# The first feed-forward block of a hybrid encoder: x loaded by token halves, the first products' operands made first, and the weight sums issued in another order

## The chip, the cores and the metric

The kernel runs on one core of a Trainium2 chip. The metric is the device time of one execution in microseconds (us), lower is better. TensorE (PE in the profile) multiplies, ScalarE (ACT) and VectorE (DVE) work elementwise, GpSimd (POOL) here only issues DMAs, and SyncE (SP) issues the plain loads.

## The reference, cut to what matters

The reference is a trunk of two layers over 512 tokens and 16 learned meta tokens (T = 528), model width 1024, float32. Each layer is half a feed-forward block, a mixer of gated linear attention and grouped-query attention, and another half block:

```python
def rmsnorm(x, g):
    xf = x.astype(jnp.float32)
    y = xf * lax.rsqrt(jnp.mean(xf * xf, axis=-1, keepdims=True) + EPS)
    return (y * g.astype(jnp.float32)).astype(x.dtype)

def swiglu(x, w_gate, w_up, w_down):
    return (jax.nn.silu(x @ w_gate) * (x @ w_up)) @ w_down
...
    for l in range(DEPTH):
        h = h + 0.5 * swiglu(rmsnorm(h, norm_gains[l, 0]),
                             ffn_w_gate[l, 0], ffn_w_up[l, 0], ffn_w_down[l, 0])
        h = h + mixer(rmsnorm(h, norm_gains[l, 1]), w_in[l], ...)
        h = h + 0.5 * swiglu(rmsnorm(h, norm_gains[l, 2]),
                             ffn_w_gate[l, 1], ffn_w_up[l, 1], ffn_w_down[l, 1])
    return rmsnorm(h, final_norm)[:, N_META:]
```

Only the start of the first `swiglu` (layer 0, block 0; the hidden width is 2816) is touched here.

## The kernel before, in words

The residual stream `h` lies in SBUF with channels on partitions: eight chunks of 128 channels by 528 tokens. Every float32 product is made of three matmuls on split values: an operand v becomes hi = v rounded to the PE's reduced float32 (a cast on ACT) and lo = v - hi (a subtraction on DVE), and hi·hi, hi·lo and lo·hi are added up in PSUM. For weights these are `whi` (line L290 of the program before, L304 after) and `wlo` (L291, L305).

Gate and up projections of a feed-forward block go by a scheme that needs seven block products instead of eight. The 22 hidden tiles of 128 form 11 pairs, the 8 chunks of channels form 4 pairs, and the 528 tokens two halves of 264. A product "(p, c)" below is product number c of hidden pair p: 24 matmuls of 128x264 (4 channel pairs, 2 columns, 3 splits). Products "1", "2" and "4" use the weight blocks W11, W12 and W22 as they are, loaded by SP; the others use sums of blocks: "7" uses s3 = W21 - W11, "6" uses s2 = W22 + s3, "5" uses s1 = W21 + W22, "3" uses s4 = s2 - W12. For the first pairs of a block (`OPENING` and those that `chained` names) the sums are made by the memory system: a negation on ACT or a plain load puts the first block into a tile of 512 KB, and an accumulating DMA that POOL issues (`add`, L209 before, L212 after) adds the other one. s2 needs s3, so its add waits for the add of s3, and s4's waits for that of s2. An engine's instructions run in the order in which they are written; an add whose tile isn't ready holds up every later add on POOL.

The products of the first block run in the order (0,1), (0,2), (1,1), (1,2), (0,4), (1,4), (0,6), (0,5), (0,7), and then (0,3), (1,6) and (1,5), of which before runs (1,6) and seven matmuls of (1,5) ahead of (0,3).

The operand side needs seven combinations of the two channel halves (b11, b12 of one chunk, b21, b22 of the other; the second index is the token half): b11 for product "1", b21 for "2", b12 - b11 and b22 - (b12 - b11) for "5" and "6", and so on, the one in place 5 for product "4". `Norm.pair` makes all seven for one channel pair in one go: two scaled copies of h (L512), the casts of the seven (L519) and their low parts (L520). The norm's division is made later: the squares of h (`square`, L502) are summed on DVE (L506), multiplied by a matrix of constants on PE (`means`, L474), and a reciprocal root follows on ACT and DVE (`rsqrt_of`); its result scales the hidden tiles (L651). `snapshot` (L605, L615) copies a PSUM accumulator to SBUF on ACT.

In before, x comes in chunk by chunk and pair by pair, with `pair(0)` to `pair(3)` and the first four weight blocks made in turn:

```python
    first.pair(0)
    W.fetch(1)
    for c in (2, 4, 6):
        nc.sync.dma_start(hall[:, c : c + 2], xt[:, c : c + 2])
    W.make(1)
    W.fetch(2)
    first.pair(1)
```

The functions that the change touches are these, with the line numbers of the profile.

Of the kernel before, what the change touches and what calls it, by code (L numbers as in the profile page):

```python
# [146 lines left out]
    return cols, -(-col // SLAB)  # L147


NPAIR = FF // P // 2  # L150
NOP = NPAIR + QUADS * FAST
PLAN = weight_plan()
# [19 lines left out]
class Weights:  # L172
# [3 lines left out]
    def __init__(self, tc, raw, hi, lo, wts, win):  # L176
        nc = tc.nc
        self.tc, self.nc, self.raw, self.hi_pool, self.lo_pool, self.wts, self.win = tc, nc, raw, hi, lo, wts, win
        self.long = self.short = None
        self.loads = []  # L180
        for t, col in zip(PLAN, COLUMN):
            if t[0] == "op":
                self.loads.append(t[1:])
            elif col % SLAB == 0:
                self.loads.append(col // SLAB)
        self.at = {load: i for i, load in enumerate(self.loads)}
        self.made, self.fetched, self.got, self.summed, self.raws = 0, 0, {}, {}, {}
        self.pos = 0
        self.behind = None

    def dram(self, f, i, name):
        return self.win[((f[0] * 2 + f[1]) * NOP + i) * 4 + ("11", "12", "21", "22").index(name)]

    def block(self, f, i, name, pool=None, tag="raw"):

        w = (pool or self.raw).tile([P, SLAB], F32, tag=tag, name=f"w{name}_{f[0]}{f[1]}_{i}")
# [9 lines left out]

    def add(self, t, src):

        self.nc.gpsimd.dma_start(t, src, accum_op=ALU.add)  # L209

    def chained(self, f, i):
        return i < 2 or f == (0, 0) and i < 4  # L212
# [1 line left out]
    def begin_sums(self, f, i, w=None):  # L214

        got = self.summed
        s3 = None
        if self.chained(f, i):
            s3 = self.negative(f, i, "s3", w)
            self.add(s3, self.dram(f, i, "21"))  # L220
        elif i < NPAIR:
            s3 = self.block(f, i, "21", self.long, "wsa")
        s2 = self.block(f, i, "22", self.short, "wsb")
        if self.chained(f, i):
            self.add(s2, s3)
        got[f, i, "7"], got[f, i, "6"] = s3, s2
        if (f, i) not in OPENING:
            self.first_sum(f, i)

    def first_sum(self, f, i):  # L230
        s1 = self.block(f, i, "21", self.short, "wsb")
# [3 lines left out]
    def sums(self, f, i, product, w):  # L235


        got, V = self.summed, self.nc.vector
        if (f, i) in OPENING and product in "12":
            (self.begin_sums if product == "1" else self.first_sum)(f, i, *[w] * (product == "1"))  # L240
        if i < 2:
            if product == "2":
                s4 = self.negative(f, i, "s4", w)
                self.add(s4, got[f, i, "6"])
                got[f, i, "3"] = s4
        elif product == "1" and not self.chained(f, i):
            if i < NPAIR:
                self.kept1 = w
            else:
                got[f, i, "7"] = self.negative(f, i, "s3", w)  # L250
                self.add(got[f, i, "7"], self.dram(f, i, "21"))
                self.add(got[f, i, "6"], got[f, i, "7"])
        elif product == "2":
            self.kept = w
            if i < NPAIR and not self.chained(f, i):
                V.tensor_tensor(got[f, i, "7"], got[f, i, "7"], self.kept1, ALU.subtract)
        elif product == "6":
            s4 = self.long.tile([P, SLAB], F32, tag="wsa", name=f"s4_{f[0]}{f[1]}_{i}")
            V.tensor_tensor(s4, w, self.kept, ALU.subtract)
            got[f, i, "3"] = s4  # L260

    def fetch(self, upto):

        while self.fetched < min(upto, len(self.loads)):
            load = self.loads[self.fetched]
            if isinstance(load, int):
                w = self.raw.tile([P, SLAB], F32, tag="raw", name=f"raw{load}")
                self.nc.sync.dma_start(w, self.wts[load])
                self.raws[self.fetched] = w
            elif load[2] in DIRECT:  # L270
                self.raws[self.fetched] = self.block(*load[:2], DIRECT[load[2]])
# [4 lines left out]
    def make(self, upto):  # L276
        nc = self.nc
        while self.made < min(upto, len(self.loads)):
            self.fetch(self.made + 1)
            s = self.made  # L280
            load = self.loads[s]
            w = self.raws.pop(s, None)
            if w is None:
                w = self.summed.pop(load)
            hi = self.hi_pool.tile([P, SLAB], F32R, tag="whi", name=f"whi{s}")
            lo = self.lo_pool.tile([P, SLAB], F32R, tag="wlo", name=f"wlo{s}")
            for a in np.split(np.arange(SLAB), 2 if s == 0 else 1):
                cs = slice(a[0], a[-1] + 1)
                with self.tc.issue_after(self.behind) if self.behind else nullcontext():
                    nc.scalar.copy(hi[:, cs], w[:, cs])  # L290
                nc.vector.tensor_tensor(lo[:, cs], w[:, cs], hi[:, cs].bitcast(F32), ALU.subtract)  # L291
            self.got[s] = (hi, lo)
            self.got.pop(s - 12, None)
            self.made += 1
            if not isinstance(load, int) and load[2] in "126":
# [36 lines left out]
def build(tc, ctx, xt, wts, win, par, w2, const, umask, out):  # L332
# [155 lines left out]
    class Norm:  # L488


        def __init__(self, gc):
            self.gc, self.x, self.acc = gc, [], None

        def operand(self, c):
            hi, lo = slot("x", F32R), slot("x", F32R)
# [12 lines left out]
        def pair(self, j):  # L508
# [23 lines left out]
            parts(slice(4, 6), v2(t34))  # L532
            self.x.append((hi, lo))

        def chunk(self, c):
            self.operand(c)
            self.square(c)
# [35 lines left out]

    pending = [load_constants]

    def ffn(l, f, norm, done, following):

        x, rs, up, n = norm.x, None, None, live[0]
        w = n // 2
# [177 lines left out]
        for i, step in enumerate(steps):  # L757
            if step[0] == "P":
                if step[1:] == (0, "5") and norm.acc is None:
                    for c in range(KC):  # L760
                        norm.square(c)
                product_of_pair(*step[1:])
                if step[1:] == (0, "5"):
                    rs, up = norm.rs(True)
                    W.behind = prev_act[0]
                if step[1] in (2, 3) and step[2] in "6574":
                    m = next(risen)
                    V.scalar_tensor_tensor(h(m), h(m), -1.0, up, ALU.mult, ALU.mult)
                if i == last_op:
                    close_pools(norm.pools)  # L770
                    following()
            elif step[0] == "S":
                fast_down(*step[1:])
            elif step[0] == "O":
                g, last = step[1:]
                ks = slice(3, 4) if last else slice(0, 3)
                operands_of(g, ks, "152")
                difference(g, 0, 3, 0, ks)
                if last:
                    operand(g, "6")  # L780
            else:
                down(*step[1:])
        close_pools(pools)

    def project(x, rs, tag, f=1.0, n=T):
# [445 lines left out]
    def ending(sums, operand, rs):  # L1231
# [43 lines left out]
        factor(1)  # L1275
        leave(1, (0, 2, 4, 6))

    first = Norm(G_NORM)
    operand_pools(first, "xc")
    bp = [block_pools()]  # L1280
    nc.sync.dma_start(h(1), xt[:, 1])
    first.pair(0)
    W.fetch(1)
    for c in (2, 4, 6):
        nc.sync.dma_start(hall[:, c : c + 2], xt[:, c : c + 2])
    W.make(1)
    W.fetch(2)
    first.pair(1)
    W.make(2)
    W.fetch(3)  # L1290
    first.pair(2)
    W.make(3)
    W.fetch(4)
    first.pair(3)
    nc.sync.dma_start(ct[:, C_O1024 : C_O1024 + P], const[:, C_O1024 : C_O1024 + P])

    norms = [first] + [Norm(G_NORM + i * KC) for i in range(1, 3 * DEPTH)]
    for l in range(DEPTH):
        a, b, c = norms[3 * l : 3 * l + 3]
        ffn(l, 0, a, b.chunk, lambda: operand_pools(b, "x"))  # L1300
# [79 lines left out]
```

## Time and profile before

| | us |
|---|---|
| median of 3 runs | 2196.76 (2196.46 to 2197.05) |
| the profiled execution, whole | 2196.04 |
| its span | 2194.3 |
| PE busy in it | 2157.0 (98%) |
| DVE busy | 1777.9 (81%) |
| ACT busy | 1215.5 (55%) |
| POOL busy | 105.3 (5%) |
| mean granted PE clock | 0.998 |

The span runs from the first to the last instruction of the profiled execution; the execution's own time is 1.7 us longer. A row of a timeline reads: start, duration, engine, line, operation, result <- operands, shapes, count, and in brackets how long the engine was idle before it and what ended that wait.

### The profile page before, as it was taken

What the parts mean: (1) busy time and instruction counts of PE and PEld (TensorE: products, weight loads), DVE (VectorE), ACT (ScalarE), POOL (GpSimd) and SP (SyncE); (2) the same over time, 40 slices, a digit from 0 to 9 for tenths busy, and PEclk for the clock granted to TensorE, in tenths of its full rate; (3) what the DMA queues carried; (4) which work ended last, traced back from release to release, by engine and by line L of the source; (5) the groups of instructions that cost most, each with busy time, mean ns of one, the idle gap of its engine ahead of it and who ended that gap; (6) DMA issues with size and microseconds to landing.
All of it is one profiled execution on the core that took longest, in us unless ns stands there. A gap on an engine that the chain in (4) does not pass through costs nothing.

```text
span 2194.3 us, 40087 instructions
## 1 busy us (share of the span) xinstructions
PE 2157.0 (98%) x16506; PEld 2066.7 (94%) x16506; DVE 1777.9 (81%) x2699; ACT 1215.5 (55%) x1781; POOL 105.3 (5%) x124
## 2 busy tenths in 40 slices
PE   7999999999999999999999999999999999999998
PEld 7999999989999999999999999999788888999997
DVE  7887977586976689788799879785878767997987
ACT  8545545354784556454575455453557836554543
POOL 1100000000000000010010000000000001000100
PEclk9999999999999999999999999999999999999999
DMA  9866743212113567676667667432121145776752
GB/s 282 218 194 184 200 125 111 78 49 68 49 39 120 129 176 182 202 182 184 165 164 186 198 181 203 127 109 80 49 78 49 49 134 151 197 202 181 195 161 68
DMA packets 87751, 312.46 MB, mean 142 GB/s; under 512 B 9744, under 2 KB 12176, under 8 KB 87568
## 3 DMA queue, kind: packets, MB, share of 16 engines
q1 hardware_dynamic: 68336, 244.48, 33.6%
q0 software_dynamic: 17280, 62.92, 16.1%
q10 hardware_dynamic: 1952, 2.50, 0.4%
q8 instruction: 130, 2.13, 0.4%
q14 instruction: 53, 0.43, 0.1%
HBM read 289.94 MB, written 2.10 MB: 133 GB/s over the span
## 4 chain that ended last, share of the span: by engine, by line
PE 76%; DVE 16%; ACT 4%; issue 2%; DMA 2%; SPq 0%; POOL 0%; DVEq 0%; ACTq 0%
PE ss L601 33%; PE mm L468 13%; PE ss L721 11%; PE ss L468 10%; DVE wlo L291 4%; PE sm L468 2%; DVE g L687 1%; PE sm L1083 1%; DVE c L683 1%; DVE g L683 1%; PE ss L1058 1%; DVE c L651 1%; DMA w<-win 1%; DVE g L661 1%; PE ss L474 1%
## 5 line engine op out<-in xcount | busy, mean ns | idle before, releaser
L601 PE MATMUL ss<-xc,whi 128*128 128x264 f32 (+1 forms) x4928 | 903.4, 285 | 11.6 <-ACT whi L290 7.4
L601 PEld LDWEIGHTS ss<-xc,whi 128*128 128x128 f32 x4928 | 764.8, 189 | 14.9 <-ACT whi L290 7.8
L601 PE MATMUL ss<-xc,wlo 128*128 128x264 f32 (+1 forms) x2464 | 700.7, 285 | 3.4 <-DVE wlo L291 3.3
L601 PEld LDWEIGHTS ss<-xc,wlo 128*128 128x128 f32 x2464 | 465.1, 189 | 5.2 <-DVE wlo L291 5.2
L291 DVE TENSOR_TENSOR wlo<-w,whi 128x1024 fp32r<-128x1024 f32 (+1 forms) x335 | 405.5, 1217 | 64.1 <-ACT whi L290 63.9
L290 ACT CAST whi<-w 128x1024 fp32r<-128x1024 f32 (+1 forms) x335 | 345.9, 1048 | 159.8 <-PE ss L601 80.3
L468 PE MATMUL mm<-x,whi 128*128 128x264 f32 (+1 forms) x1712 | 384.8, 315 | 0.0
L468 PEld LDWEIGHTS mm<-x,whi 128*128 128x128 f32 x1712 | 278.4, 188 | 16.6 <-issue 1.0
L468 PE MATMUL mm<-x,wlo 128*128 128x264 f32 (+1 forms) x856 | 266.1, 315 | 0.0
L721 PE MATMUL ss<-g,whi 128*128 128x264 f32 (+1 forms) x1280 | 237.0, 284 | 0.0
L290 ACT CAST whi<-raw 128x1024 fp32r<-128x1024 f32 x126 | 132.1, 1049 | 163.5 <-PE mm L468 102.7
L605 ACT COPY c<-ss 128x528 f32<-128x528 f32 (+1 forms) x132 | 78.5, 595 | 245.7 <-PE ss L601 245.3
L291 DVE TENSOR_TENSOR wlo<-raw,whi 128x1024 fp32r<-128x1024 f32 x126 | 153.9, 1222 | 59.3 <-ACT whi L290 58.4
L721 PEld LDWEIGHTS ss<-g,whi 128*128 128x128 f32 x1280 | 198.4, 188 | 0.1
L721 PE MATMUL ss<-g,wlo 128*128 128x264 f32 (+1 forms) x640 | 181.3, 283 | 0.0
L468 PEld LDWEIGHTS mm<-x,wlo 128*128 128x128 f32 x856 | 159.6, 188 | 8.5 <-issue 0.7
L468 PE MATMUL ss<-g,whi 128*128 128x264 f32 (+2 forms) x900 | 166.2, 299 | 0.0
L468 PEld LDWEIGHTS ss<-g,whi 128*128 128x128 f32 x900 | 131.7, 188 | 5.2
L209 POOL DMA_DIRECT2D w<-win x60 | 52.7, 879 | 1557.1 <-DVE t L1211 392.2
L721 PEld LDWEIGHTS ss<-g,wlo 128*128 128x128 f32 x640 | 120.5, 188 | 0.0
L447 ACT ACTIVATE c<-c 128x528 f32<-128x528 f32 (+1 forms) x88 | 56.5, 642 | 96.3 <-DVE c L651 96.1
L291 DVE TENSOR_TENSOR wlo<-s,whi 128x1024 fp32r<-128x1024 f32 x86 | 104.9, 1220 | 1.7 <-ACT whi L290 1.5
(268 smaller groups left out, 3374.0 us busy)
## 6 DMA issues: line engine op xcount, KB each, us to landing
w<-win SPq DMA_DIRECT2D x333, 512.0 KB, 4.5
raw<-wts SPq DMA_DIRECT2D x126, 512.0 KB, 3.3
w<-win POOLq DMA_DIRECT2D x60, 512.0 KB, 7.4
s<-win POOLq DMA_DIRECT2D x26, 512.0 KB, 7.6
w<-s POOLq DMA_DIRECT2D x26, 512.0 KB, 6.0
s<-w POOLq DMA_DIRECT2D x8, 512.0 KB, 8.0
h<-xt SPq DMA_DIRECT2D x3, 528.0 KB, 6.6
out<-h ACTq DMA_DIRECT2D x4, 256.0 KB, 2.4
```

What stands on the lines that cost most here:

```text
L209: self.nc.gpsimd.dma_start(t, src, accum_op=ALU.add)
L290: nc.scalar.copy(hi[:, cs], w[:, cs])
L291: nc.vector.tensor_tensor(lo[:, cs], w[:, cs], hi[:, cs].bitcast(F32), ALU.subtract)
L447: prev_act[0] = S.activation(*args, **kw).ins
L468: TE.matmul(acc.half[i][:width], lhs, rhs[:, acc.spans[i]], start=first, stop=last)
L474: TE.matmul(a, weights, x[:, hs], start=True, stop=True)
L601: TE.matmul(acc[:, j], a[:, j, k], b[:, at], start=bool(begin and k == 0 and i == 0), stop=k == len(x) - 1 and i == 2, skip_group_check=no ...
L605: W.behind = S.copy(part(st, q), acc).ins
L651: V.scalar_tensor_tensor(td, ts, -0.5, rs[:, cs], ALU.mult, ALU.mult)
L661: V.tensor_tensor(raw[p // 4][2 * m + q][:, p % 4], t[:, q * w : (q + 1) * w], us, ALU.mult)
L683: V.tensor_tensor(lo, src[:, ks], hi.bitcast(F32), ALU.subtract)
L721: TE.matmul(acc[:, j], a[:, j, k], xs[b][:, k], start=bool(begin and k == 0 and i == 0), stop=k == 3 and i == 2, skip_group_check=not begin)
```

## The change

Four things are changed, all at the program's start.

- x is loaded by token halves: the first half of channels 0 and 1, then of the others, then the second halves. `Norm.pair` is replaced for this block: `head(j)` makes the operands of products "1" and "2" of a pair (from the first half of the tokens, two half-width activations that are the cast themselves), `fourth(j)` that of product "4", `middle(j)` and `rest(j)` the others. The heads of all four pairs come first; the others are called from `between`, after given steps of the product loop.
- Three early blocks (W12 of pair 1, W22 of pairs 0 and 1) go into spare tiles of another pool ("g"), and W22 of pair 0 for the second sum is loaded ahead, behind x.
- The sums of the two opening pairs are made by `open_sums`, with the second add kept ahead of the next pair's first one (`issue_after`); the negations are made when products "1" and "2" are.
- `warm_up(5)` runs five float32 matmuls on a tile of zeros ahead of everything.

```diff
@@ class Weights
+    def open_sums(self, f, i):
+        got = self.summed
+        with self.tc.issue_after(self.added) if self.added else nullcontext():
+            self.add(got[f, i, "7"], self.dram(f, i, "21"))
+        s2 = got[f, i, "6"] = self.second.pop((f, i), None) or self.block(f, i, "22", self.short, "wsb")
+        self.added = self.add(s2, got[f, i, "7"]).ins
+        self.first_sum(f, i)
+        self.add(got[f, i, "3"], s2)
...
-        if (f, i) in OPENING and product in "12":
-            (self.begin_sums if product == "1" else self.first_sum)(f, i, *[w] * (product == "1"))
-        if i < 2:
+        if (f, i) in OPENING:
+            if product in "12":
+                name, into = ("s3", "7") if product == "1" else ("s4", "3")
+                got[f, i, into] = self.negative(f, i, name, w)
+        elif i < 2:
@@ the program's start
-    nc.sync.dma_start(h(0), xt[:, 0])
+    nc.sync.dma_start(hall[:, 0:2, :HF], xt[:, 0:2, :HF])
...
+    def warm_up(n):
+        z = slot("rs")
+        V.memset(z, 0.0)
+        into = pair()
+        for i in range(n):
+            TE.matmul(into[:, i % 2, :HF], z[:, :P], z[:, P : P + HF], start=True, stop=True)
@@ class Norm
+        def head(self, j):
+            hi, lo = self.tiles()
+            for i in range(2):
+                src, g = h(2 * j + i, slice(0, live[0] // 2)), col(self.gc + 2 * j + i)
+                scaled_in = S.activation(hi[:, i], src, AF.Identity, scale=g).ins
+                V.scalar_tensor_tensor(lo[:, i], src, g, hi[:, i].bitcast(F32), ALU.mult, ALU.subtract)
+            return scaled_in
...
+        def fourth(self, j):
+            w = live[0] // 2
+            raw, t, fourth = twin("g"), v2(slot("t")), slot("t")[:, :w]
+            for i in range(2):
+                S.activation(raw[:, i], h(2 * j + i), AF.Identity, scale=col(self.gc + 2 * j + i))
...
+            self.parts(j, 5, fourth)
@@ the first block
+    W.spare = slots["g"]
     W.fetch(1)
+    load_x(2, 2, halves[0])
+    load_x(4, 4, halves[0])
     W.fetch(4)
+    load_x(0, 4, halves[1])
+    load_x(4, 4, halves[1])
+    W.second[(0, 0), 0] = W.block((0, 0), 0, "22", W.short, "wsb")
+    W.fetch(6)
+    W.behind = first.head(0)
+    W.make(1, False)
+    W.behind = None
+    for j in range(1, KC // 2):
+        first.head(j)
+    W.sums((0, 0), 0, "1", W.last)
...
+    begin = [lambda i=i: W.open_sums((0, 0), i) for i in range(2)]
+    between = {0: each(first.fourth, range(2)), 1: each(first.fourth, range(2, 4)) + begin[:1], 3: begin[1:] + each(first.middle),
+               4: each(first.rest)}
```

The order in which things are issued changes with it. First POOL, whose queue holds all the adds: these are its first eight before. `s3_00_0` is the sum s3 of pair 0, `w22_00_0` the tile that becomes s2, `w21_00_0` the one that becomes s1, `s4_00_0` s4, and `00_1` is pair 1; `win` is the weights in memory.

```order
L209 DMA s3_00_0_134<-win 128x1024
L209 DMA w22_00_0_137<-s3_00_0_134 128x1024
L209 DMA w21_00_0_168<-win 128x1024
L209 DMA s4_00_0_171<-w22_00_0_137 128x1024
L209 DMA s3_00_1_202<-win 128x1024
L209 DMA w22_00_1_205<-s3_00_1_202 128x1024
L209 DMA w21_00_1_276<-win 128x1024
L209 DMA s4_00_1_279<-w22_00_1_205 128x1024
```

And the same eight places after the change:

```order
L212 DMA s3_00_0_156<-win 128x1024
L212 DMA w22_00_0_120<-s3_00_0_156 128x1024
L212 DMA s3_00_1_176<-win 128x1024
L212 DMA s4_00_0_170<-w22_00_0_120 128x1024
L212 DMA w21_00_0_279<-win 128x1024
L212 DMA w22_00_1_346<-s3_00_1_176 128x1024
L212 DMA w21_00_1_349<-win 128x1024
L212 DMA s4_00_1_230<-w22_00_1_346 128x1024
```

s3 of pair 1 has moved from the fifth place to the third, and s1 of pair 0, which product (0,5) uses, from the third to the fifth.

Second, ACT, around the weight of product (0,5), `whi7`. Before, the squares of the norm (L502) stand between the casts of the weights:

```order
L290 CAST whi6_370<-w22_00_0_137 128x1024
L502 ACTIVATE t36_473<-h_82 128x528
L290 CAST whi7_411<-w21_00_0_168 128x1024
L502 ACTIVATE t37_476<-h_82 128x528
L502 ACTIVATE t38_479<-h_82 128x528
L502 ACTIVATE t39_482<-h_82 128x528
L290 CAST whi8_440<-s3_00_0_134 128x1024
```

After, with `xc` an operand's tile, `c` a snapshot and `s4_00_1` the negation of W12 of pair 1, the squares are at L524:

```order
L304 CAST whi7_427<-w21_00_0_279 128x1024
L681 COPY c29_313<-ss36_426 128x2x264
L559 CAST xc5_138<-t33_408 128x264
L304 CAST whi8_456<-s3_00_0_156 128x1024
L559 CAST xc7_144<-t34_414 128x264
L559 CAST xc9_150<-t35_420 128x264
L671 COPY c12_202<-ss11_165 128x2x264
L524 ACTIVATE t37_487<-h_82 128x528
L524 ACTIVATE t38_489<-h_82 128x528
```

Copies and all eight squares now stand behind the cast of `whi7`, and with them three casts that `rest` makes.

More of the change, by code (lines that the diff above doesn't have):

```diff
@@ L188, in __init__ @@
         self.pos = 0
-        self.behind = None
+        self.behind = self.spare = self.added = None
+        self.second = {}
     def dram(self, f, i, name):
@@ L270, in fetch @@
             elif load[2] in DIRECT:
-                self.raws[self.fetched] = self.block(*load[:2], DIRECT[load[2]])
+                self.raws[self.fetched] = self.block(*load[:2], DIRECT[load[2]], *[self.spare, "g"] * (load in SPARE))
                 if load[2] == "1" and load[:2] not in OPENING:
@@ L274, in fetch, with make @@
             self.fetched += 1
-    def make(self, upto):
+    def make(self, upto, summing=True):
         nc = self.nc
@@ L294, in make @@
             self.made += 1
-            if not isinstance(load, int) and load[2] in "126":
+            self.last = w
+            if summing and not isinstance(load, int) and load[2] in "126":
                 self.sums(*load, w)
@@ L533, in pair, with parts, tiles, middle @@
             self.x.append((hi, lo))
+        def parts(self, j, at, src):
+            hi, lo = self.x[j]
+            S.copy(hi[:, at], src)
+            V.tensor_tensor(lo[:, at], src, hi[:, at].bitcast(F32), ALU.subtract)
+        def tiles(self):
+            w = live[0] // 2
+            self.x.append([slots["xc"].tile([P, 7 * T // 2], F32R, tag="xc", name=nm("xc"))[:, : 7 * w]
+                           .rearrange("p (s c) -> p s c", s=7) for _ in range(2)])
+            return self.x[-1]
+        def head(self, j):
[6 more added lines that the diff above has]
+        def fourth(self, j):
+            w = live[0] // 2
+            raw, t, fourth = twin("g"), v2(slot("t")), slot("t")[:, :w]
+            for i in range(2):
+                S.activation(raw[:, i], h(2 * j + i), AF.Identity, scale=col(self.gc + 2 * j + i))
+            b11, b12, b21, b22 = [raw[:, i, a : a + w] for i in range(2) for a in (0, w)]
+            V.tensor_tensor(t[:, 0], b12, b11, ALU.subtract)
+            V.tensor_tensor(t[:, 1], b22, t[:, 0], ALU.subtract)
+            V.tensor_tensor(fourth, b21, t[:, 1], ALU.subtract)
+            self.parts(j, 5, fourth)
+            self.left.append((t, b12, b22))
+        def middle(self, j):
+            self.parts(j, slice(2, 4), self.left[j][0])
+        def rest(self, j):
+            (hi, lo), (_, b12, b22) = self.x[j], self.left[j]
+            third = slot("t")[:, : live[0] // 2]
+            V.tensor_tensor(third, b12, b22, ALU.subtract)
+            self.parts(j, 4, third)
+            S.activation(hi[:, 6], b22, AF.Copy, scale=-1.0)
+            V.scalar_tensor_tensor(lo[:, 6], b22, -1.0, hi[:, 6].bitcast(F32), ALU.mult, ALU.subtract)
         def chunk(self, c):
@@ L574, in build, with ffn @@
     pending = [load_constants]
-    def ffn(l, f, norm, done, following):
+    def ffn(l, f, norm, done, following, between={}):
         x, rs, up, n = norm.x, None, None, live[0]
@@ L782, in ffn @@
                 down(*step[1:])
+            for call in between.get(i, ()):
+                call()
         close_pools(pools)
@@ L1299, in build @@
         a, b, c = norms[3 * l : 3 * l + 3]
-        ffn(l, 0, a, b.chunk, lambda: operand_pools(b, "x"))
+        ffn(l, 0, a, b.chunk, lambda: operand_pools(b, "x"), between if l == 0 else {})
         close_pools(bp.pop())
```

28 lines of the change are left out of this document (11 added, 17 removed).

## The prediction

> **What bounds the kernel now.** I began with the page's chain of waits and its DMA queues.
>
> ```profile
> PE 76%; DVE 16%; ACT 4%; issue 2%; DMA 2%; SPq 0%; POOL 0%; DVEq 0%; ACTq 0%
> ...
> q1 hardware_dynamic: 68336, 244.48, 33.6%
> q0 software_dynamic: 17280, 62.92, 16.1%
> ```
>
> The first row gives three quarters of the chain to TensorE (PE). The other two say what one 512 KB transfer costs when it has all 16 DMA engines: 33.6% of 2194.3 us over 244.48 MB is 1.58 us for a plain load, 16.1% over 62.92 MB is 2.94 us for an accumulating one. Next come the windows of PE (us, PE busy with its instructions, clock, DMA share, GB/s).
>
> ```profile
> 0.00:7.41 7.41, 0.00 (x1) 1.00 0.77 247
> 7.41:18.97 11.56, 8.89 (x30) 1.00 1.03 354
> 18.97:26.89 7.92, 6.42 (x45) 1.00 1.06 292
> 26.89:38.65 11.76, 11.76 (x96) 1.00 1.04 294
> 38.65:47.00 8.35, 6.91 (x53) 1.00 1.03 222
> 52.00:66.00 14.00, 13.77 (x113) 1.00 1.02 266
> 130.00:200.00 70.00, 70.00 (x576) 1.00 0.64 191
> ```
>
> From about 66 us on PE is full, so whatever is won or lost earlier moves the whole rest and is neither repaid nor multiplied. Idle PE time before that is 7.4 + 2.7 + 1.5 + 1.4 + 0.2 us, and the DMA engines are full (1.02 to 1.06) through the same stretch. The list of waits for the first 90 us names what PE waited for most (us in total, times, longest):
>
> ```profile
> PE ss L601 <- ACT whi L290: 7.4, 1, 7.4
> ...
> PE ss L474 <- ACT whi L290: 1.4, 1, 1.4
> ```
>
> PE loses most before its first matmul, and 1.4 us at the means of the norm. In PE's own timeline the pace changes once, although the granted clock reads 1.00 throughout:
>
> ```profile
> 18.31 0.64 PE L601 MATMUL ss<-xc,whi 128*128 128x264 f32 x2
> 18.75 0.42 PE L601 MATMUL ss<-xc,wlo 128*128 128x264 f32 x1
> 18.97 0.51 PE L601 MATMUL ss<-xc,whi 128*128 128x264 f32 x2
> ```
>
> Three matmuls start over 0.66 us here, 0.22 each. That is the pace until about 19 us; afterwards 96 of them fill 11.76 us in the window above, 0.122 each.
>
> **The early part of the change.** These rows carry the start of before, and the length of a whole cast (1.0), a full-width scaling or square (0.57) and a copy out of PSUM (0.6); then a wlo on DVE:
>
> ```profile
> 4.01 1.36 ACT L512 ACTIVATE t<-h,par 128x528 f32<-128x528 f32 x2 [1.99 <-DMA par<-par]
> 5.28 0.71 ACT L519 CAST xc<-t 128x264 fp32r<-128x264 f32 x2
> ...
> 32.17 1.70 ACT L502 ACTIVATE t<-h 128x528 f32<-128x528 f32 x3
> 33.78 1.04 ACT L290 CAST whi<-s 128x1024 fp32r<-128x1024 f32 x1
> 34.72 0.59 ACT L615 COPY c<-ss 128x528 f32<-128x528 f32 x1
> ```
>
> ```profile
> 29.86 1.23 DVE L291 TENSOR_TENSOR wlo<-w,whi 128x1024 fp32r<-128x1024 f32 x1 [1.27 <-ACT whi L290]
> ```
>
> Half a pair is now made in two half-width activations of about 0.4 us each and needs no other part of x. ACT still starts at 4.0 with the parameters, and one half of the weight's cast follows (0.5 us): first matmul at 5.4, against 7.4. W12's whi comes after the next pairs' heads, near 10.3, its wlo (1.2 us) at 11.5, and about 70 matmuls of the first four products are left. At 0.122 us they end at 20.0; were the slow pace to last 11.6 us from the first matmul, as before, 25 of them at 0.22 would move this to 22.5. Both lie ahead of the next step. The five matmuls on zeros are of the kind in the row at 40.44 below, 0.4 us each or 0.7 at the slow pace: 2 to 3.5 us from about 1.5, over by 5.0 on a PE that has nothing else. They cost nothing, and a pace that rises sooner wins nothing while (0,4) comes at 23.6; without that cover it would be worth up to the 2.5 us between 20.0 and 22.5. The spare buffers let loads go sooner that PE doesn't wait for last.
>
> Product (0,4) needs the fourth operand of each pair, and ACT makes it in order from 9.3 us: three casts and two negations (of a cast's size) at 1.0, one copy of 0.6, eight scalings at 0.6 and three short casts at 0.36 make 11.5 us, to 21.0 with a short wait between, then whi of this product at 22.1 and its wlo at 23.6. From there 72 matmuls, (0,4), (1,4), (0,6), run together and end at 23.6 + 72 x 0.122 = 32.4. In before the same point is where PE falls idle, 1.45 us ahead of 40.44 in the row below. So the start wins 6.6 us to here, if the second add, on which (0,6) rests, lands by 28; it lands then as before, near 26.
>
> ```profile
> 40.44 1.13 PE L474 MATMUL ss<-t,const 128*128 128x264 f32 x4 [1.45 <-ACT whi L290]
> 41.22 0.59 PE L601 MATMUL ss<-xc,whi 128*128 128x264 f32 x2
> ...
> 46.89 0.41 PE L601 MATMUL ss<-xc,whi 128*128 128x264 f32 x2
> ```
>
> **The queue of adds.** Every weight sum is an accumulating load on POOL's one queue, and the order on it changes. POOL's timeline of before:
>
> ```profile
> 9.17 1.01 POOL L209 DMA_DIRECT2D s<-win  x1 [8.72 <-ACT s L204]
> 19.01 0.87 POOL L209 DMA_DIRECT2D w<-s  x1 [8.83 <-DMA s<-win]
> ...
> 26.01 0.89 POOL L209 DMA_DIRECT2D s<-w  x1 [5.24 <-ACT whi L290]
> 26.55 1.25 POOL L209 DMA_DIRECT2D s<-win  x1
> 36.70 0.87 POOL L209 DMA_DIRECT2D w<-s  x1 [8.90 <-DMA s<-win]
> ```
>
> The first add takes 9.8 us. The second, which must have it, goes at 19.0; the third, 0.5 us behind, is s1 of pair 0, the operand of (0,5). The fourth and fifth go at 26.0 and 26.6, and the fifth has landed at 36.7, when the sixth, which waits for it, goes. The changed order makes s3 of pair 1 the third and s1 of pair 0 the fifth. The negation starts about 1 us earlier (first add near 8.2, done by 18), but W22 of pair 0 now arrives behind the whole of x, so the second add goes near 18.9, hardly sooner. The fifth slot therefore keeps its time and (0,5) gets its operand there. Call that landing L. The nearest row says 36.7; more plain loads are queued by then, and with one of them taking half of its 1.6 us in this add's way I put L = 37.6. The bounds: issue at 26.0 plus this row of the page,
>
> ```profile
> w<-win POOLq DMA_DIRECT2D x60, 512.0 KB, 7.4
> ```
>
> gives 33.4; 36.7 plus two plain loads of 1.58 gives 39.9. The Trainium skill, page "DMA: Bandwidth & Descriptors", section "Queues, rings and completion order", says that a DMA engine takes the queues in turn, packet by packet. By that rule a plain load that is always waiting takes half the engine, an add alone would need twice 2.94 us, and two in flight 11.8 (an estimate): L = 37.8 and the end 0.2 us later; the fifth add's 10.1 us in the trace, between 2.94 and 11.8, leans to its side.
>
> **What follows L.** ACT is done with everything ahead by 29 and stands, in order, at the cast of s1. Its work behind that is made of casts, copies and squares, whose rows stand above; DVE's sums of squares have this one:
>
> ```profile
> 36.46 3.88 DVE L506 TENSOR_TENSOR t<-t,t 128x528 f32<-128x528 f32 x5
> ```
>
> ACT: two whi at 1.0, two copies at about 0.55, three short casts at 0.3 end at L + 4.0; then eight squares at 0.55 and a negation, to L + 9.2. In before the squares at 32.17 ran while PE was busy; now they queue behind L. DVE can make wlo of (0,5) only after the low parts that those casts release: L + 5.1. PE, which has done four matmuls of (0,5) and (0,7), then runs 44 more to L + 10.5. DVE's seven sums of squares (about 0.74 each) begin at L + 6.3, with one wlo (1.2) among them, and end at L + 12.6. The two means matmuls stand ahead of (0,3) on PE; they took 41.22 - 40.44 = 0.8 us, so (0,3) begins at L + 13.7 = 51.3. The matching point of before, the first matmul after (0,5) and (0,7), is 15 triples past 41.22, the row at 46.89: **+4.4 us**.
>
> The reciprocal root then has three activations, the third as long as the second of these rows:
>
> ```profile
> 41.61 0.70 ACT L480 ACTIVATE rs<-ss,eps 128x528 f32<-128x528 f32 x1 [1.39 <-PE ss L474]
> 42.34 0.65 ACT L447 ACTIVATE rs<-rs 128x528 f32<-128x528 f32 x1
> ```
>
> From the means' start at L + 12.6 = 50.2 it is 1.2 to the first activation (41.61 - 40.44), 0.7 for each of the three, 0.6 for each of two DVE steps and 1.2 for the wlo that stands behind them: 55.9. PE has done the 24 matmuls of (0,3) and two more at 54.5, a wait of 1.4. The scaling that follows puts an activation on ACT that waits for the hidden sums on DVE, and the cast of a weight behind it: PE, at 122 ns a matmul, comes to that weight about 0.9 early by the same count. Against these stand the 0.3 us that before idles between 47 and 66 (0.1 and 14.00 - 13.77). Sum: 4.4 + 1.4 + 0.9 - 0.3 = **+6.4 us**, and in general L - 31.2. On the profiled execution, 2196.04 us (span 2194.3), that is 2202.4; the runs shown have their median, 2196.76, 0.7 above it, so 2203.1. A difference under 0.2%, 4.4 us, is about what a measurement of this kernel can't tell from none: the lines are 2192.4 and 2201.2.
>
> **Rivals.**
>
> 1. The adds run quicker, because the loads of x are done and less is in their way: fourth and fifth 2.94 us apart from 26 on give L = 31.9, the bound above 33.4, and L - 31.2 makes +0.7 to +2.2: 2197.5 to 2199.0, same. For it: the DMA share falls after 66 us. Against: it reads 1.04 and 1.03 in the windows from 26.89 to 47.00. Chance 0.22.
> 2. PE's slow pace comes back. Between 32.4 and L + 5.1 = 42.7 PE has four matmuls to do, and before has no such hole once it is warm: its 1.45 us did not change the pace. If the 44 matmuls go at 0.22, they end at L + 14.8, 2.2 us behind the sums of squares, and the means and (0,3) shift by it: up to +3 with the first of (0,3) slow too. If the pace recovers after the first 15, the 1.5 us lost hides in the 2.1 us that PE waits for the sums. In the middle +1.4: 2204.5, chance 0.27, slower. The Trainium skill, page "TensorE: Matmul & The Clock Gate", section "Part 1: The HAM clock gate", states the rule: half clock after an idle window of about 3.4 us, full clock after a busy one. By it the fallback comes for certain and the price is nearly nil; the trace's 11.6 us at the slow pace, PE 77% busy, differs from its 3.4.
> 3. The start's gain stays. If (0,5)'s operand is there by 28, PE never stops, and the 6.6 us at (0,6) go through to the end: 2190. It needs adds at 1 us each after 26, or the change to do on the chip what its words say of the first sum: its load is ahead, but by the written order its add is not. Chance 0.09.
>
> **How the numbers follow.** The forecast has 0.42; 2203.1, with 2199.0 to 2205.5 from the bounds of L, 33.4 and 39.9. About 0.08 of it lies under 2201.2. The range takes in rival 1 and the dear end of rival 2, and from each one plain load's 1.6 us further: 2197.5 - 1.6 = 2195.9, and 2203.1 + 3 + 1.6 = 2207.7. It leaves out rival 3. Faster: 0.08 of rival 3. Same: 0.22 + 0.08 + 0.01 = 0.31. Slower: 0.34 + 0.27 = 0.61.
>
> **What would show it.** In the changed profile: first matmul at 5.3 to 5.6; (0,6) ended by 32 to 33; then a PE wait on ACT's whi that DMA released, with the cast of s1 starting at 37 to 38; (0,3) first at 50 to 52. If the cast of s1 starts under 34, the queue's price is wrong and rival 1 holds. If matmuls after the hole lie 0.22 us apart for longer than 15, rival 2. If (0,6) ends past 35, the early part is wrong too, and the loss would be no larger, since L sets the rest. The forecast as a whole falls if PE has no wait over 3 us between 25 and 45.

## The result, and the profile after

The changed kernel takes 2205.14 us (median of 6, 2203.3 to 2207.14) against 2197.27 for the kernel before on the same chips (6 runs): 7.9 us more, a ratio of 1.0036 with a 95% interval of 1.0025 to 1.0047. The profiled execution took 2205.42 us, its span 2203.6. The forecast, 2203.1 in a range of 2195.9 to 2207.7, has the sign and most of the size.

PE's timeline of the changed kernel, the rows where a step begins or a wait ends:

```profile
1.50 4.77 PE L433 MATMUL ss<-rs 128*128 128x264 f32 x10 [1.50 <-DVE rs L430]
5.70 0.92 PE L667 MATMUL ss<-xc,whi 128*128 128x264 f32 x2
...
20.84 0.28 PE L667 MATMUL ss<-xc,wlo 128*128 128x264 f32 x1
23.16 0.59 PE L667 MATMUL ss<-xc,whi 128*128 128x264 f32 x2 [2.03 <-ACT whi L304]
24.81 0.59 PE L667 MATMUL ss<-xc,wlo 128*128 128x264 f32 x1 [1.07 <-DVE wlo L305]
...
40.29 0.65 PE L667 MATMUL ss<-xc,whi 128*128 128x264 f32 x2 [4.27 <-ACT whi L304]
...
51.92 1.13 PE L496 MATMUL ss<-t,const 128*128 128x264 f32 x4 [0.65 <-PE ss L667]
53.61 0.48 PE L667 MATMUL ss<-xc,whi 128*128 128x264 f32 x2 [0.56 <-DVE c L693]
...
57.82 0.39 PE L667 MATMUL ss<-xc,wlo 128*128 128x264 f32 x1 [0.79 <-DVE wlo L305]
...
67.54 0.39 PE L667 MATMUL ss<-xc,wlo 128*128 128x264 f32 x1 [0.45 <-DVE wlo L305]
```

The first row is the five matmuls on zeros. The start is 1.7 us earlier, (0,6) ends at 40.29 - 4.27 = 36.0 against 38.6 (in before three matmuls of (0,5) follow it ahead of the wait at 39.0), and then PE waits for `whi7`, the weight of (0,5). (0,3) begins at 53.6, where before had its next product at 46.9. ACT's row for that weight in before, then in the changed kernel, and there POOL's first six adds:

```profile
31.23 1.03 ACT L290 CAST whi<-w 128x1024 fp32r<-128x1024 f32 x1
```

```profile
39.19 1.04 ACT L304 CAST whi<-w 128x1024 fp32r<-128x1024 f32 x1 [6.96 <-DMA w<-win]
```

```profile
8.78 1.00 POOL L212 DMA_DIRECT2D s<-win  x1 [8.33 <-ACT s L207]
19.67 0.87 POOL L212 DMA_DIRECT2D w<-s  x1 [9.89 <-DMA w<-win]
20.20 1.22 POOL L212 DMA_DIRECT2D s<-win  x1
29.14 0.89 POOL L212 DMA_DIRECT2D s<-w  x1 [7.71 <-DMA w<-s]
29.68 1.26 POOL L212 DMA_DIRECT2D w<-win  x1
33.02 0.86 POOL L212 DMA_DIRECT2D w<-s  x1 [2.08 <-DMA s<-win]
```

ACT stood 7 us at that cast. Its operand's add was issued fifth, at 29.68, and landed at 39.1: that is L. The windows of PE (us, PE busy with its instructions, clock, DMA share, GB/s):

```profile
20.00:26.00 6.00, 2.90 (x17) 0.79 1.05 360
26.00:33.00 7.00, 7.00 (x44) 0.70 1.06 286
33.00:38.00 5.00, 3.02 (x25) 1.00 1.07 215
38.00:41.00 3.00, 0.65 (x2) 0.92 0.97 273
41.00:47.00 6.00, 3.51 (x14) 0.50 0.35 59
47.00:52.00 5.00, 4.35 (x35) 0.97 1.02 254
52.00:66.00 14.00, 12.66 (x97) 1.00 0.73 159
...
130.00:200.00 70.00, 70.00 (x575) 1.00 0.57 171
```

The waits that set PE back are all before 68 us, and in the window from 130 us PE is as full as before. The first matmul of the block's down projection, which comes behind all the products above, shows how far the rest is shifted; first of before, then of the changed kernel:

```profile
100.45 0.40 PE L721 MATMUL ss<-g,whi 128*128 128x264 f32 x2
```

```profile
108.38 0.40 PE L787 MATMUL ss<-g,whi 128*128 128x264 f32 x2
```

That is 7.9 us. The two profiled executions differ by 9.4: another 1.4 arise later, between 220 and 980 us. Experiment 3, the changed kernel but for its zeros, doesn't have them, so I don't count them to the change; where they come from was not looked into.

The granted clock falls twice, to means of 0.79 and 0.70 between 20 and 33 us and to 0.50 between 41 and 47: the slow pace came back. Last, the DMAs issued in the stretch from 18 to 40 us (line, operation, count, KB each, median us from issue to landing), of before:

```profile
w<-win SPq DMA_DIRECT2D x6, 512.0 KB, 6.5
w<-s POOLq DMA_DIRECT2D x2, 512.0 KB, 6.6
w<-win POOLq DMA_DIRECT2D x2, 512.0 KB, 8.9
```

and of the changed kernel:

```profile
w<-win SPq DMA_DIRECT2D x3, 512.0 KB, 15.0
w<-s POOLq DMA_DIRECT2D x2, 512.0 KB, 9.1
s<-win POOLq DMA_DIRECT2D x1, 512.0 KB, 12.5
```

Adds and plain loads are both longer in flight.

### The profile page after: what moved, and what is told of

The parts are those of the page before. It is cut to its first block, busy times and chain, and to the rows that moved or that the text cites. A ratio compares the mean times of both kernels' runs of the same rounds, so it can differ in the third digit from the quotient of the medians.

```text
span 2203.6 us, 40117 instructions
## 1 busy us (share of the span) xinstructions
PE 2162.8 (98%) x16516; PEld 2070.3 (94%) x16516; DVE 1780.0 (81%) x2704; ACT 1216.3 (55%) x1785; POOL 105.0 (5%) x124
## 4 chain that ended last, share of the span: by engine, by line
PE 73%; DVE 17%; ACT 4%; DMA 3%; issue 3%; SPq 0%; DVEq 0%; POOL 0%; ACTq 0%; POOLq 0%
PE ss L667 31%; PE mm L490 12%; PE ss L787 10%; PE ss L490 9%; DVE wlo L305 4%; PE sm L490 2%; DMA w<-win 2%; DVE g L753 1%; PE sm L1151 1%; DVE c L749 1%; DVE g L749 1%; DMA w<-s 1%; DVE c L717 1%; PE ss L1126 1%; DVE g L727 1%
## 5 line engine op out<-in xcount | busy, mean ns | idle before, releaser
L667 PE MATMUL ss<-xc,whi 128*128 128x264 f32 (+1 forms) x4928 | 904.7, 285 | 12.6 <-ACT whi L304 7.1
L490 PE MATMUL ss<-g,wlo 128*128 128x264 f32 (+2 forms) x450 | 106.2, 300 | 0.0
```

Of the source, the lines that this page charges most:

```text
L490: TE.matmul(acc.half[i][:width], lhs, rhs[:, acc.spans[i]], start=first, stop=last)
L667: TE.matmul(acc[:, j], a[:, j, k], b[:, at], start=bool(begin and k == 0 and i == 0), stop=k == len(x) - 1 and i == 2, skip_group_check=no ...
```

## The experiments

Two theories stood against each other. The **queue theory** is the prediction's: the end follows L, the landing of s1 of pair 0, because that add went from POOL's third place to its fifth; ACT, DVE and PE queue behind it. The **pace theory** is its second rival grown larger: PE's clock, which falls in the new holes, costs the time. All times below are medians; the ratio is to before on the same chip.

**1. s1 third again** (e1_s1_third): the changed kernel with the add put back.

```diff
-        self.added = self.add(s2, got[f, i, "7"]).ins
-        self.first_sum(f, i)
-        self.add(got[f, i, "3"], s2)
+        self.add(s2, got[f, i, "7"])
+        self.added = self.first_sum(f, i)      # returns the add
+        with self.tc.issue_after(self.added):
+            self.add(got[f, i, "3"], s2)
```

> The changed kernel with the accumulating load of s1 of pair 0 (the operand of product (0,5)) put back into the third place of POOL's queue, ahead of s4 of pair 0 and s3 of pair 1; all else as in the changed kernel. Queue theory (the end follows the landing L of that operand): the cast of whi7 starts at 31 to 34 instead of 39.2, the wait of PE at (0,5) falls from 4.3 us to under 2, and the time returns to about that of before, 2195 to 2200; not much under it, since s3 of pair 1 is now fifth, as in before, and product (1,6) can't start earlier than there. Pace theory (the fall of PE's clock from 20 us on is what costs): the clock falls at 21 to 25 as well, and the time stays at 2202 or more.

Measured: 2199.82, 1.0013 (1.0004 to 1.0022). ACT's row at the weight of (0,5), and PE's at the means:

```profile
32.99 1.05 ACT L305 CAST whi<-w 128x1024 fp32r<-128x1024 f32 x1 [0.93 <-DMA w<-win]
```

```profile
45.73 1.13 PE L497 MATMUL ss<-t,const 128*128 128x264 f32 x4 [1.99 <-issue]
```

L falls by 6.2 us and the time by 5.3. The clock fell in this run too (0.76 in the window from 26 to 33). So the queue's order alone carries two thirds of the 7.9 us. What is left is 2.8 over before. PE waits 2 us at the means, which start at 45.7 against 40.4 in before because the squares still come late, and the clock falls behind that wait (0.57 from 47 to 50 us). That the squares cost these 2.8 us is not shown: in experiment 7, with s1 out of the way, moving them ahead did not lower the time.

**2. Only the order of the adds, in the kernel before** (e2_before_s1_fifth).

```diff
 def first_sum(self, f, i):
-        self.add(s1, self.dram(f, i, "22"))
+        if (f, i) == ((0, 0), 0):
+            self.later = s1
+        else:
+            self.add(s1, self.dram(f, i, "22"))
 def begin_sums(self, f, i, w=None):
-            self.add(s3, self.dram(f, i, "21"))
+            third = self.add(s3, self.dram(f, i, "21")).ins
+            if (f, i) == ((0, 0), 1):
+                with self.tc.issue_after(third):
+                    self.add(self.later, self.dram(f, 0, "22"))
```

> The kernel before with one thing of the change alone: on POOL's queue s1 of pair 0 goes fifth, behind s3 of pair 1, instead of third. Queue theory: the cast of whi7 moves from 31.2 to 36.5 to 39, the squares behind it on ACT move with it, the means on PE from 40.4 to about 45, and the time rises by 4 to 6, to 2201 to 2203. If the rest of the change is what costs (x in halves, operands in pieces, the clock), the time stays within 1.5 of before.

Measured: 2204.77, 1.0040 (1.0027 to 1.0053): 7.7 us more than before, 2 to 4 more than I expected.

```profile
38.69 1.05 ACT L296 CAST whi<-w 128x1024 fp32r<-128x1024 f32 x1 [6.90 <-DMA w<-win]
```

```profile
42.83 0.51 PE L607 MATMUL ss<-xc,whi 128*128 128x264 f32 x2 [2.40 <-ACT c L621]
47.47 2.10 PE L480 MATMUL ss<-t,const 128*128 128x264 f32 x4 [4.00 <-ACT whi L296]
```

The one move, with x, operands and start as they were, costs what the whole change costs. The excess over what I expected is in the last row: the means start at 47.5, not 45, and take 2.10 us instead of 1.13, at the half clock. PE has no wait behind them up to 110 us, so nothing there hides the slow matmuls.

**3. Without the five matmuls on zeros** (e3_no_zeros).

```diff
-    warm_up(5)
```

> The changed kernel without its five matmuls on zeros. Queue theory: the first products run slower for longer, (1,2) ends up to 2.5 us later, still ahead of the operand of (0,4) or within 1 us of it, and L is unchanged: 2204 to 2206.5, the changed kernel's time. Pace theory: the time moves by 2 us or more, upward if the zeros keep the clock up.

Measured: 2206.40, 1.0044 (1.0031 to 1.0056): not told apart from the changed kernel. PE's rows:

```profile
23.66 0.51 PE L667 MATMUL ss<-xc,whi 128*128 128x264 f32 x2 [2.03 <-ACT whi L304]
25.32 0.39 PE L667 MATMUL ss<-xc,wlo 128*128 128x264 f32 x1 [1.15 <-DVE wlo L305]
39.73 0.81 PE L667 MATMUL ss<-xc,whi 128*128 128x264 f32 x2 [5.63 <-ACT whi L304]
```

It says more than was asked. In this execution the hole at 21 to 25 did not drop the clock (the matmul at 25.32 takes 0.39, not 0.59), so (0,6) ended at 39.73 - 5.63 = 34.1, 1.9 us earlier than in the changed kernel. PE then waited 1.4 longer for the same weight, which came 0.6 earlier, and the down projection starts at 108.0 instead of 108.4. So the slow pace ahead of L cost at most 0.4 us of the 1.9.

**4. The pace held up by extra matmuls** (e4_pace_kept).

```diff
+            busy = {"4": 24, "5": 64}.get(product, 0) if (l, f, p) == (0, 0, 0) else 0
+            for i in range(busy):
+                TE.matmul(acc[:, i % 2], prior[0][:, 0, 0], x[0][0][:, prior[1]], start=True, stop=True)
```

> The changed kernel with extra matmuls in the two holes of PE, 24 ahead of product (0,4) and 64 ahead of (0,5); they write into the accumulator that the product then starts anew, so nothing else changes. Queue theory: matmuls stay 0.12 us apart and the clock at 1.00, (0,6) ends at 33 to 34 instead of 36, the operand of (0,5) still lands at 39, the means still wait for DVE's sums at about 51.9, and the time moves by less than 1: 2204 to 2206. Pace theory: the 72 matmuls from (0,4) on save 2.5 us and the 44 after the hole 1.6, and the time falls to 2201 to 2202.5.

Measured: 2208.65, 1.0055 (1.0041 to 1.0069): 3.5 slower than the changed kernel, outside both expectations.

```profile
51.89 2.10 PE L496 MATMUL ss<-t,const 128*128 128x264 f32 x4 [6.38 <-issue]
```

The run did not test what it was for. With the extra matmuls the scheduler placed the means ahead of 38 matmuls of (0,5) and (0,7) instead of behind them, and PE stood 6.4 us in front of them with that work queued behind; the clock fell there, and the means went at the slow pace. One thing can be read from it: the means come at 51.9, as in the changed kernel, though PE stood idle ahead of them; it is DVE's sums behind L that set them, and these end at 51.8 here.

**5. The squares ahead of `whi7`** (e5_squares_first).

```diff
-               4: each(first.rest)}
+               4: [lambda c=c: first.square(c) for c in range(KC)] + each(first.rest)}
```

> The changed kernel with the eight squares of the norm issued on ACT ahead of the cast of whi7 instead of behind it; the queue of adds is left as it is. PE then has the means after the second matmul of (0,5), and (1,6) with seven matmuls of (1,5) ahead of (0,3), as in before. Queue theory with the term of the squares (they stand behind L and put DVE's sums, the means, the root and (0,3) 2 to 3 us behind the end of (0,7)): L stays at 39, PE goes on without a stop after (0,7), and the time falls by 3 to 5, to 2200 to 2202. If that term was wrong and only L counts, the time falls by less than 1.5.

Measured: 2202.58, 1.0026 (1.0016 to 1.0036), 2.6 under the changed kernel: between the two expectations.

```profile
40.27 0.81 PE L667 MATMUL ss<-xc,whi 128*128 128x264 f32 x2 [6.37 <-ACT whi L304]
45.59 0.59 PE L667 MATMUL ss<-xc,wlo 128*128 128x264 f32 x1 [2.70 <-DVE wlo L305]
```

There is no wait at the means any more, but the wlo of (0,5) comes 1.3 us later than in the changed kernel (45.59 against 44.30), and the matmuls from there are slow. The squares' place, with the order that PE gets by it, is worth about 2.6 by the medians, not 3 to 5. That is a loose figure: the intervals of the two kernels overlap (1.0016 to 1.0036 and 1.0025 to 1.0047), and in the profiles the down projection starts only 1.1 us earlier (107.25 against 108.38).

**6. s1 by DVE, no add at all** (e6_s1_by_vector).

```diff
-        self.first_sum(f, i)
+        if i:
+            self.first_sum(f, i)
+        else:
+            self.addends = self.block(f, i, "21", self.short, "wsb"), self.raws[self.at[f, i, "4"]]
...
+    def sum_by_vector(self):
+        s1, w22 = self.addends
+        with self.tc.issue_after(self.low):
+            self.nc.vector.tensor_tensor(s1, s1, w22, ALU.add)
+        self.summed[(0, 0), 0, "5"] = s1
-               4: each(first.rest)}
+               4: [W.sum_by_vector] + each(first.rest)}
```

> The changed kernel with s1 of pair 0 not made by an add on POOL's queue at all: DVE adds the plain blocks W21 and W22, which are there by then, in one 128x1024 addition (1.2 us). Queue theory: the cast of whi7 no longer waits for a DMA, it starts at 33 to 36, and the time falls by 5 to 7, to 2198 to 2200, about before's; it does not fall under before, since the squares still stand behind on ACT and the means come at 43 to 46. If the queue is not what binds (pace, or x in halves), the time stays at 2203 or more.

Measured: 2198.23, 1.0003 (0.9995 to 1.0012).

```profile
33.98 1.05 ACT L313 CAST whi<-w 128x1024 fp32r<-128x1024 f32 x1
```

```profile
46.26 1.13 PE L505 MATMUL ss<-t,const 128*128 128x264 f32 x4 [0.45 <-PE ss L676]
```

The cast no longer waits for a DMA, and about 7 of the 7.9 us are gone. It is the clearest of the runs, with one reservation: it also takes an entry off POOL's queue, so a later add, s1 of pair 1, goes at 41.3 instead of 43.5.

**7. Both** (e7_vector_and_squares), the edits of 5 and 6 together.

> Both at once: s1 of pair 0 by DVE as in the run before this one, and the eight squares ahead of the operands of rest() and of whi7. Queue theory: the means no longer stop PE behind (0,7), product (0,3) no longer waits for them, and the time is at or a little under before's, 2194 to 2198. If something else of the change costs, for instance its start, it stays 2 or more above before.

Measured: 2198.44, 1.0006 (0.9997 to 1.0015): a little over the range, and no better than the run before. PE's clock falls here too; run 9 asks whether that is why.

**8. Without the spare tiles** (e8_no_spare).

```diff
-SPARE = ((0, 0), 1, "2"), ((0, 0), 0, "4"), ((0, 0), 1, "4")
+SPARE = ()
```

> The changed kernel without the spare tiles: W12 of pair 1 and W22 of pairs 0 and 1 wait for tiles of their own pool, so that fewer plain loads are under way while the adds run. If the plain loads that the spare tiles let go early are what makes the adds long (9.1 and 12.5 us in the stretch from 18 to 40 us against 6.6 and 8.9 before), the second add lands 1 to 2 us sooner and L falls from 39.1 to 37 to 38, but (0,4) gets its weight later: the time is within 1.5 of the changed kernel's. If they do not matter for the adds, L stays at 39 or more and the time rises by 0 to 2.

Measured: 2206.78, 1.0044 (1.0032 to 1.0057). Its DMAs from 18 to 40 us, and its POOL rows:

```profile
w<-win SPq DMA_DIRECT2D x3, 512.0 KB, 7.6
w<-s POOLq DMA_DIRECT2D x2, 512.0 KB, 8.2
s<-win POOLq DMA_DIRECT2D x1, 512.0 KB, 10.6
```

```profile
20.79 0.87 POOL L212 DMA_DIRECT2D w<-s  x1 [10.93 <-DMA w<-win]
...
28.48 0.89 POOL L212 DMA_DIRECT2D s<-w  x1 [5.93 <-DMA w<-s]
```

With fewer plain loads under way the second add took 7.7 us (20.79 to 28.48, when the next add goes) instead of 9.5 (19.67 to 29.14), and the third 10.6 instead of 12.5. In the other runs that keep the spare tiles and the first three adds in this order, the second took 9.2 to 9.6. L fell by 1.0, to 38.2 by the start of the cast of `whi7`: less than expected, because the second add had been issued 1.1 later. The time is 1.6 above the changed kernel's, just outside what I expected. The early loads of the spare tiles do lengthen the adds, but letting them wait gains nothing.

**9. Run 7 with PE kept busy in its holes** (e9_pace_on_path): 16 extra matmuls ahead of (0,4), 14 ahead of (0,5), 15 ahead of the means, 17 behind them, each into an accumulator that starts anew.

> The kernel with s1 by DVE and the squares ahead, with extra matmuls that keep PE busy in its holes: 16 ahead of (0,4), 14 ahead of (0,5), 15 ahead of the means and 17 behind them, all into accumulators that are started anew afterwards. Without them the granted clock fell to 0.50 between 38 and 46 us, just when PE had become the bound, and about 20 matmuls went at 0.22 instead of 0.122. If the pace costs what those matmuls say, the clock stays at 1.00 from 36 to 47 and the time falls by 1.5 to 2.5, to 2196 to 2197, a little under before's. If the pace is hidden there too, the time stays at 2198.4 or rises by the extra matmuls, up to 2.

Measured: 2195.98, 0.9998 (0.9989 to 1.0007). PE's windows of run 7:

```profile
38.00:41.00 3.00, 2.29 (x6) 0.65 0.47 169
41.00:47.00 6.00, 5.20 (x29) 0.61 0.73 159
```

and of this run, extra matmuls among them:

```profile
38.00:41.00 3.00, 3.00 (x24) 1.00 0.47 169
41.00:47.00 6.00, 6.00 (x51) 1.00 0.61 128
```

29 matmuls against 51 in the same 6 us; 11 of the 51 are extra ones, so the kernel's own are 40. The median is 2.5 lower, against before on the same chip 1.8, but the two intervals overlap. And the traces don't put the gain where the pace was: these are the first matmuls of the down projection, of run 7 and of this run.

```profile
101.88 0.40 PE L796 MATMUL ss<-g,whi 128*128 128x264 f32 x2
```

```profile
102.27 0.40 PE L809 MATMUL ss<-g,whi 128*128 128x264 f32 x2
```

With the clock up, (0,7) ended 1.3 us earlier (47.9 against 49.2), but PE then waited for a weight whose load had not landed, and at 102 us this run is no longer ahead. Its span is 1.2 us shorter (2195.4 against 2196.6), and that arises later. So the price of the pace in run 7 is not shown; in these two executions the next late operand took back what it won.

**10. W22 of the second sum ahead of x's second halves** (e10_w22_ahead), on top of run 9.

```diff
+    W.second[(0, 0), 0] = W.block((0, 0), 0, "22", W.short, "wsb")
     load_x(0, 4, halves[1])
     load_x(4, 4, halves[1])
-    W.second[(0, 0), 0] = W.block((0, 0), 0, "22", W.short, "wsb")
```

> The same, with the load of W22 of pair 0 for the second sum put ahead of the second halves of x instead of behind them. In the changed kernel the second add waited for this load until 19.7. Queue theory: the second add goes at 17.5 to 18.5, lands 1 to 2 sooner, the cast of the weight of (0,6) no longer waits for it, and the time is 0 to 1.5 under the run before this one. If x's second halves were needed just as early, the operands of (0,4) come later by up to 1.6 and the time rises by up to 1.5.

Measured: 2196.57, 0.9998 (0.9989 to 1.0006).

```profile
18.32 0.87 POOL L212 DMA_DIRECT2D w<-s  x1 [7.83 <-DMA s<-win]
```

The second add goes at 18.3 and now waits for the first add, not for the load, and the adds behind it go 1.5 earlier; but the cast of the weight of (0,4) comes 1.5 later (23.65 against 22.19), as the other branch of the expectation had it. The time is that of run 9. Runs 9 and 10 are the lowest medians, but neither is told apart from before: the earlier start and the earlier products are there, and yet the end is before's. I take it that ACT and DVE, which must make the same operands in less time, now set it: from 27 to 42 us of run 9 DVE is busy for 13.6 and ACT for 13.5 of the 15 us, against 12.8 and 12.1 in before. No run here took work from them alone, and the late load in run 9 is another candidate, so that stays an inference.

## Why the prediction was right, and by how much each step was off

- **Start**: first matmul 5.4 forecast, 5.70 measured. (1,2) done at 20.0 forecast, 21.0 measured (20.84 and one pace). Right within 1 us.
- **Zeros and pace of the first products**: no cost to the end, no gain, as said; experiment 3 bears it out. But the zeros were not over by 5.0: they took 4.77 us from 1.50, not 2 to 3.5. The first matmul comes at 5.70 with them and at 5.50 without.
- **Fourth operands**: wlo of (0,4) at 23.6 forecast, 24.8 measured; its whi came at 23.1, not 22.1, behind a wait of 0.8 us of ACT's short casts for DVE's subtractions, where I had counted only "a short wait".
- **(0,6) done** at 32.4 forecast, 36.0 measured. 1.2 of the 3.6 is the step above, the rest the half clock from 23 to 30, after a hole that I had not looked at: rival 2 put the fall behind (0,6), and it came there as well. By the prediction's own sign (past 35) the early part was wrong. Of the 6.6 us that the start was to win up to here, 2.6 were there; the 39.0 that I compared with is three matmuls behind the end of (0,6) in before. By the prediction's own sentence, L sets the rest, and experiment 3 agrees: 1.9 us more or less here moved the down projection by 0.4.
- **L**: 37.6 forecast in bounds of 33.4 to 39.9, 39.1 measured. It is as near as that because two errors went opposite ways. The second add, which I had landing "as before, near 26", landed near 29: it went at 19.67 (18.9 forecast) and was longer under way. So the fifth add was issued 3.1 later than I had it, at 29.68 instead of 26.55. Against that it took 9.5 us, about the 10.1 of before, where my 37.6 had given it 11.0. I had taken the spare tiles as something that lets loads go sooner and no more; experiment 8 shows that this lengthens the adds.
- **From L on**: means at L + 12.6 forecast, L + 12.8 measured; (0,3) at L + 13.7 forecast, L + 14.5 measured. The forecast's own terms, L + 12.6 and 0.8 for the means, give L + 13.4; the means came 0.2 later, took 1.13 and were followed by a wait of 0.56 for DVE to be done with an accumulator (L693). Against before: 53.6 - 46.9 = 6.7, not 4.4; 1.5 of the difference is L.
- **Waits behind**: 1.4 and 0.9 forecast, 0.79 and 0.45 measured. Sum of the measured terms: 6.7 + 0.8 + 0.45 - 0.3 = 7.7, against 7.9 at the down projection and 7.9 between the medians.

So the mechanism was the forecast's: the landing of s1 in the fifth place, and ACT, DVE and PE in order behind it. Its sum, 6.4, was 1.3 short of the measured terms, mainly by L; that L was not further off, and that the wrong early part did not matter to the end, were in part luck. Rival 1 (quicker adds) fell: they were slower. Rival 2's mechanism occurred but its price, 1.4, was not paid in the changed kernel: the pace recovered after some 15 matmuls, the case in which the prediction had the loss hidden, and PE, which ended (0,7) at 51.3, still waited 0.65 for the sums. The Trainium skill, page "TensorE: Matmul & The Clock Gate", section "Part 1: The HAM clock gate", has the pace recover after a busy window of about 3.4 us; behind the hole at 40 to 44 it recovered 3.0 us after PE was at work again (44.30 to 47.3), near that figure, and behind the hole at 21 to 25 only 5.1 us after (24.81 to 29.9). Rival 3 would have needed L at 28; with s1 by DVE (experiment 6) the landing is out of the way, and the gain still did not appear: the means came at 46.3, behind the squares on ACT, against 40.4 in before. With the squares ahead as well (experiment 7) they came at 38.7, and the time was still not under before's; what holds it there is open.

## What to carry to other kernels

Count what a reordering does to each in-order queue, the one that only issues DMAs too: two places back on a queue whose entries took 6 to 12 us cost 7.7 us by itself (experiment 2), more than everything that the change won. When an operand is that late, look at what stands behind its cast on the casting engine; here eight squares that could have run in a 7 us wait stood behind it, and moving them ahead was worth about 2.6 us (experiment 5), though nothing any more once the operand came early (experiment 7). And where both blocks lie in SBUF anyway, an elementwise addition of 1.2 us can take the place of an add on the DMA queue (experiment 6).

## What the runs showed of the hardware

- A hole of 3.7 us with two matmuls in it (21.1 to 24.8 in the changed kernel) was followed by the half clock there and in experiments 1 and 6, and not in experiment 3, where it was as long. One of 3.3 us was followed by it in experiment 7 and not in experiment 5. It can't be counted on either way.
- The slow pace at the program's start isn't in the granted clock (1.00 from 7 to 19 us in before, at 0.22 us a matmul), while later falls are (0.50). Without the zeros it lasted 7.4 us of PE work without a hole (5.5 to 12.9 in experiment 3); with them the kernel's own matmuls were at 0.122 from 7.9 us on.
- A 512 KB accumulating load takes 2.94 us of all engines by its packets, but with another add and plain loads in flight 5.8 to 12.5 us to its landing (adds issued between 18 and 40 us, before and after), and it moved by 2 us with three plain loads let go earlier.
